# Two operand tiles of a two-layer block move behind two others, and every product operand starts at a multiple of 512 bytes

## The chip, the cores and the metric

The kernel runs on one core of one Trainium2 chip. The metric is the device time of one execution in microseconds (us). The engines are TensorE (PE: matrix products; PEld: its loads of the stationary operand), VectorE (DVE), ScalarE (ACT), GpSimd (POOL) and SyncE (SP, which here issues the DMAs). SBUF is the on-chip memory from which the engines read; a tile takes the same range of bytes in each of its 128 partitions, and "byte n" below means byte n of each partition.

## The reference, cut to what matters

Two layers, each a mixer (recurrence, two kinds of attention) and a gated feed-forward part, over 256 tokens of width 2048:

```python
for l in range(DEPTH):                                # 2
    h = rmsnorm(x, g_mix[l])
    proj = h @ w_in[l]                                # 2048 -> 3904
    ...                                               # out_a, out_b, out_c from proj
    x = x + concatenate([out_a, out_b, out_c]) @ w_out[l]
    h = rmsnorm(x, g_ffn[l])
    x = x + (silu(h @ w_gate[l]) * (h @ w_up[l])) @ w_down[l]   # 2048 -> 5632 -> 2048
return rmsnorm(x, g_final)
```

All inputs are float32. The weights are read once, 387 MB in all.

## The kernel before

**Products.** A float32 product is made of three products of a reduced type (F32R): each operand is split into a high part, rounded to that type, and a low part, the rest. `mm3` (L207) issues the three: high by high (L209), high by low (L210 or L211) and low by high. Each is a load of a 128x128 stationary operand and a stream of 512 (or 256, 320, 384) columns of the moving operand. TensorE's order is written out by hand (`manual_schedule`); the other engines' work is ordered by a scheduler around it.

**The operands.** Weights come by DMA from SP into `wraw` (three buffers of 4,096 bytes), `load_split` (L186) has ACT write the high part `whi` (L203) and DVE the low part `wlo` (L204), three buffers of 4,096 bytes each. The activations lie transposed, split in the same way, in one of two pairs: `xTh` and `xTl` (16 slices of 1,024 bytes each, one for 128 rows of width; written by `build_xT` at L292 and L293) hold the normed input of w_in, w_gate and w_up; `hTh` and `hTl` (six buffers of 4,096 bytes each) hold the mixer's output for w_out and the hidden units for w_down.

**Who is stationary.** In `gemm` (L213) a 128x128 slice of xT or hT is stationary and 512 columns of `whi` or `wlo` move. In `gemm_T` (L253) a 128x128 slice of `whi` or `wlo` is stationary and 256 columns of xT or hT move. In the profile the moving tile is named first: `acc<-whi,xTh` has `whi` moving and `xTh` stationary.

**The loop.** The feed-forward part takes 11 blocks of 512 hidden units: for each, w_gate and w_up are read in loads of 512 KB (two slices of 128 rows by 512 columns), and each load feeds 12 products of 512 columns. After blocks 6 and 11, w_down is read in loads of 512 KB (128 rows by 1024 columns), which feed 12 products of 512 columns too. Between these products stand a few transposes on TensorE (L283).

**Where tiles lie.** Pools are laid out one behind the other in the order in which they are opened: `const`, `wraw`, `whl` (`whi`, `wlo`), `ht` (`hTh`, `hTl`), `sm`. Within `const` tiles lie in the order of their allocation, each begun at a multiple of 32 bytes. `xTh` and `xTl` are tiles of `const`, behind `half` and ahead of a 68,240 byte work area (`arena`).

Of the kernel before, what the change touches and what calls it, by code (L numbers as in the profile page):

```python
# [11 lines left out]
F32 = mybir.dt.float32  # L12
F32R = mybir.dt.float32r
# [8 lines left out]
P = 128  # L22
D = 2048
T = 256
NT = 2
DEPTH = 2
KD = D // P
# [27 lines left out]
def body(ctx: ExitStack, tc: tile.TileContext, x_in, pos_in, pvec_in, lamv_in, cst_in, w_in, w_r, w_i, w_q_b,  # L55
         w_kv_b, w_out, w_gate, w_up, w_down, g_final, out):
    nc = tc.nc
    pool = lambda name, bufs=1, **k: ctx.enter_context(tc.tile_pool(name=name, bufs=bufs, **k))
    const = pool("const")
    wraw_p = pool("wraw", 3)  # L60
    whl_p = pool("whl", 3)
    ht_p = pool("ht", 6)
    sm_p = pool("sm", 4)
    acc_p = pool("acc", 5, space=PSUM)
    aux_p = pool("aux", 3, space=PSUM)
# [11 lines left out]
    load_x(0, 256)  # L77
    nc.sync.dma_start(pv, pvec_in)

    half = const.tile([P, 8], F32, name="half")  # L80
    xTh = const.tile([P, KD, T], F32R, name="xTh")
    xTl = const.tile([P, KD, T], F32R, name="xTl")
    junk = const.tile([P, 512], BF16, name="junk")
    warm = const.tile([P, 512], BF16, name="warm")
    nc.vector.memset(warm, 0.0)
    nc.gpsimd.memset(half, -0.5)
    nc.scalar.activation(junk[:, 0:8], half, AF.Exp)
    pos_i = const.tile([P, NT], I32, name="pos_i")
    cst = const.tile([P, 40], F32, name="cst")
    rsb = const.tile([P, T], F32, name="rsb")  # L90
# [833 lines left out]
```

## Time and profile before

| | |
|---|---|
| time, three runs | 2161.57, 2165.28, 2165.72 us; median 2165.28 us |
| profiled execution: its own time | 2164.01 us |
| profiled execution: its span | 2162.2 us |
| PE busy | 2146.5 us (99% of the span) |
| DVE, ACT, POOL busy | 1157.1, 1003.4, 12.9 us |
| mean DMA rate | 181 GB/s |

The span runs from the first to the last instruction of the program; the time has 1.8 us more around it. PE's busy time counts a product from its start to its modelled end. Products overlap: one of 512 columns is shown as 0.39 us long, but the next starts about 0.23 us after it. So what TensorE takes for a product is read from the distance between starts, and a mean duration serves to compare products of the same shape.

### The profile page before, as it was taken

The numbers are of one execution on the slowest core, as the hardware profiler recorded it, in microseconds if no ns is written. First come the engines' busy times: TensorE is split into PE (matmuls) and PEld (weight loads), VectorE is DVE, ScalarE is ACT, GpSimd is POOL, SyncE is SP. The second block draws the span as 40 slices with busy tenths as digits, with TensorE's granted clock in tenths as the row PEclk, the third lists the DMA queues.
The fourth block names the chain that finished last, engine by engine and source line by source line (L and its number), as shares of the span: only waits on it lengthen the run. The fifth ranks groups of instructions, "written<-read, shape, count | busy, mean of one in ns | idle before, by whom it ended". The sixth has DMA issues, their size and how long they took to land.

```text
span 2162.2 us, 26714 instructions
## 1 busy us (share of the span) xinstructions
PE 2146.5 (99%) x10302; PEld 1783.7 (82%) x10302; DVE 1157.1 (54%) x1497; ACT 1003.4 (46%) x1345; POOL 12.9 (1%) x27
## 2 busy tenths in 40 slices
PE   9999999999999999999999999999999999999998
PEld 8888888888888888888898888888888888888886
DVE  5775755444444444444565757554444444445454
ACT  5764654444443344443447546454444433444443
POOL 0000000000000000000000000000000000000000
PEclk9999999999999999999999999999999999999999
DMA  7564456666665666666565645566666666666655
GB/s 216 172 166 131 151 176 185 185 185 184 185 189 192 193 186 186 185 186 191 181 189 158 180 126 184 178 179 190 182 185 187 191 193 189 186 187 181 189 184 171
DMA packets 183439, 391.14 MB, mean 181 GB/s; under 512 B 19088, under 2 KB 36624, under 8 KB 183184
## 3 DMA queue, kind: packets, MB, share of 16 engines
q1 hardware_dynamic: 183312, 389.45, 60.7%
q8 instruction: 80, 1.31, 0.3%
q14 instruction: 47, 0.39, 0.1%
HBM read 387.30 MB, written 2.10 MB: 180 GB/s over the span
## 4 chain that ended last, share of the span: by engine, by line
PE 98%; DMA 0%; issue 0%; ACT 0%; DVE 0%; SPq 0%; DVEq 0%; POOLq 0%; POOL 0%; ACTq 0%
PE acc L209 31%; PE acc L211 31%; PE acc L210 31%; PE aux L283 2%; PE aux L676 1%; PE aux L675 1%; PE aux L732 1%; DMA wraw<-in_w_in 0%; PE aux L690 0%; PE aux L534 0%; PE aux L533 0%; ACT whi L203 0%; PE aux L691 0%; SPq L75 0%; DVE wlo L204 0%
## 5 line engine op out<-in xcount | busy, mean ns | idle before, releaser
L204 DVE TENSOR_TENSOR wlo<-wraw,whi 128x1024 fp32r<-128x1024 f32 (+2 forms) x756 | 895.4, 1185 | 880.1 <-ACT whi L203 879.0
L203 ACT CAST whi<-wraw 128x1024 fp32r<-128x1024 f32 (+2 forms) x756 | 770.1, 1019 | 1053.4 <-PE acc L211 934.5
L209 PE MATMUL acc<-whi,xTh 128*128 128x512 f32 x1728 | 685.1, 396 | 1.8 <-ACT whi L203 1.0
L210 PE MATMUL acc<-wlo,xTh 128*128 128x512 f32 x1728 | 676.8, 392 | 0.6 <-DVE wlo L204 0.6
L211 PE MATMUL acc<-whi,xTl 128*128 128x512 f32 x1728 | 676.8, 392 | 0.0
L209 PE MATMUL acc<-whi,hTh 128*128 128x512 f32 (+1 forms) x992 | 388.6, 392 | 0.0
L209 PEld LDWEIGHTS acc<-whi,xTh 128*128 128x128 f32 x1728 | 326.1, 189 | 74.8 <-issue 1.3
L211 PEld LDWEIGHTS acc<-whi,xTl 128*128 128x128 f32 x1728 | 325.8, 189 | 73.4
L211 PE MATMUL acc<-whi,hTl 128*128 128x512 f32 (+1 forms) x992 | 385.5, 389 | 0.0
L210 PEld LDWEIGHTS acc<-wlo,xTh 128*128 128x128 f32 x1728 | 326.2, 189 | 71.4 <-DVE wlo L204 0.9
L210 PE MATMUL acc<-wlo,hTh 128*128 128x512 f32 (+1 forms) x992 | 384.8, 388 | 0.0
L209 PEld LDWEIGHTS acc<-whi,hTh 128*128 128x128 f32 x992 | 186.8, 188 | 38.1 <-issue 1.3
L211 PEld LDWEIGHTS acc<-whi,hTl 128*128 128x128 f32 x992 | 186.5, 188 | 38.0
L210 PEld LDWEIGHTS acc<-wlo,hTh 128*128 128x128 f32 x992 | 186.8, 188 | 36.9
L209 PE MATMUL acc<-xTh,whi 128*128 128x256 f32 x384 | 110.6, 288 | 0.2 <-ACT whi L203 0.2
L211 PE MATMUL acc<-xTh,wlo 128*128 128x256 f32 x384 | 108.4, 282 | 0.8 <-DVE wlo L204 0.8
L210 PE MATMUL acc<-xTl,whi 128*128 128x256 f32 x384 | 108.2, 282 | 0.6 <-DVE xTl L293 0.6
L209 PEld LDWEIGHTS acc<-xTh,whi 128*128 128x128 f32 x384 | 72.4, 188 | 2.7 <-issue 1.3
L210 PEld LDWEIGHTS acc<-xTl,whi 128*128 128x128 f32 x384 | 72.4, 189 | 1.1 <-DVE xTl L293 1.0
L211 PEld LDWEIGHTS acc<-xTh,wlo 128*128 128x128 f32 x384 | 72.3, 188 | 1.2 <-DVE wlo L204 1.2
L826 DVE SCALAR_TENSOR_TENSOR arena<-acc,rs,arena 128x512 f32<-128x512 f32 x44 | 32.9, 748 | 42.9 <-PE acc L211 42.9
L283 PE MATMUL aux<-ident,arena 128*128 128x128 f32 x324 | 48.6, 273 | 0.0
(174 smaller groups left out, 868.1 us busy)
## 6 DMA issues: line engine op xcount, KB each, us to landing
wraw<-in_w_gate SPq DMA_DIRECT2D x176, 512.0 KB, 3.7
wraw<-in_w_up SPq DMA_DIRECT2D x176, 512.0 KB, 3.7
wraw<-in_w_down SPq DMA_DIRECT2D x176, 512.0 KB, 4.5
wraw<-in_w_out SPq DMA_DIRECT2D x64, 512.0 KB, 3.8
wraw<-in_w_in SPq DMA_DIRECT2D x64, 384.0 KB, 3.2
wraw<-in_w_in SPq DMA_DIRECT2D x48, 512.0 KB, 3.8
wraw<-in_w_in SPq DMA_DIRECT2D x32, 416.0 KB, 3.4
wraw<-in_w_q_b SPq DMA_DIRECT2D x8, 384.0 KB, 4.0
```

Of the source, the lines that this page charges most:

```text
L203: nc.scalar.copy(hi[:, :n], raw[:, :n])
L204: nc.vector.tensor_tensor(lo[:, :n], raw[:, :n], hi[:, :n].bitcast(F32), ALU.subtract)
L209: nc.tensor.matmul(ps, a[0], b[0], start=start, stop=False)
L210: nc.tensor.matmul(ps, a[0], b[1], start=False, stop=False)
L211: nc.tensor.matmul(ps, a[1], b[0], start=False, stop=stop)
L283: nc.tensor.transpose(ps[:, d:d + P], s, ident)
L675: nc.tensor.matmul(S[:, c0:c0 + n], qT[:, h, qs], kT[:, h, 0:n], start=True, stop=False)
L676: nc.tensor.matmul(S[:, c0:c0 + n], qrT[b0:b0 + 64, h // 2, qs], krT[b0:b0 + 64, 0:n], start=False, stop=True)
L732: nc.tensor.matmul(S[:, c0:c0 + n], qk[b0:b0 + 64, 0, q * P:(q + 1) * P], qk[b0:b0 + 64, 1, 0:n], start=True, stop=True)
L826: nc.vector.scalar_tensor_tensor(sil[t], ps, rs[0][:, t:t + 1], sil[t], ALU.mult, ALU.mult)
```

## The change

`xTh` and `xTl` leave `const` for a pool of their own, `xt`, which is opened behind `ht` and ahead of `sm`. `half` is allocated two tiles later, and a new tile `pad` of 32 bytes is allocated in `const` and set to zero on POOL.

```diff
     ht_p = pool("ht", 6)
+    xt_p = pool("xt")
     sm_p = pool("sm", 4)
...
-    half = const.tile([P, 8], F32, name="half")
-    xTh = const.tile([P, KD, T], F32R, name="xTh")
-    xTl = const.tile([P, KD, T], F32R, name="xTl")
+    xTh = xt_p.tile([P, KD, T], F32R, name="xTh")
+    xTl = xt_p.tile([P, KD, T], F32R, name="xTl")
     junk = const.tile([P, 512], BF16, name="junk")
     warm = const.tile([P, 512], BF16, name="warm")
     nc.vector.memset(warm, 0.0)
+    half = const.tile([P, 8], F32, name="half")
     nc.gpsimd.memset(half, -0.5)
     nc.scalar.activation(junk[:, 0:8], half, AF.Exp)
+
+    pad = const.tile([P, 8], F32, name="pad")
+    nc.gpsimd.memset(pad, 0.0)
```

The built programs place the tiles as follows (first byte of the first buffer; the buffers of one name follow each other at multiples of 4,096 bytes, and all slices that a product reads begin at multiples of 512 bytes within them):

| tile | before | rest of 512 | after | rest of 512 |
|---|---|---|---|---|
| `xTh` | 34,144 | 352 | 192,512 | 0 |
| `xTl` | 50,528 | 352 | 208,896 | 0 |
| `arena` | 70,176 | 32 | 37,440 | 64 |
| `wraw` | 139,232 | 480 | 106,496 | 0 |
| `whi` | 151,520 | 480 | 118,784 | 0 |
| `wlo` | 163,808 | 480 | 131,072 | 0 |
| `hTh` | 176,096 | 480 | 143,360 | 0 |
| `hTl` | 200,672 | 480 | 167,936 | 0 |

On PE, DVE, ACT and SP the two programs have the same instructions in the same order. POOL has one more. At the start of the program POOL's rows before are, with `ident` the unit matrix for the transposes and `arena` the work area:

```order
masks.py:197 MEMSET ident 128x128
L86 MEMSET half 128x8
L455 MEMSET arena 128x6x3
masks.py:199 ISA
masks.py:199 AFFINE_SELECT ident<-ident 128x128
```

and of the changed kernel:

```order
masks.py:197 MEMSET ident 128x128
L87 MEMSET half 128x8
L91 MEMSET pad 128x8
L459 MEMSET arena 128x6x3
masks.py:199 ISA
masks.py:199 AFFINE_SELECT ident<-ident 128x128
```

The zeroing of `pad` stands ahead of the last step of `ident`.

## Rows read from the trace of the kernel before

**Rows 1.** The page: busy us, share of the span and instructions of each engine.
```profile
PE 2146.5 (99%) x10302; PEld 1783.7 (82%) x10302; DVE 1157.1 (54%) x1497; ACT 1003.4 (46%) x1345; POOL 12.9 (1%) x27
```

**Rows 2.** The page: the chain that ended last, shares of the span by engine.
```profile
PE 98%; DMA 0%; issue 0%; ACT 0%; DVE 0%; SPq 0%; DVEq 0%; POOLq 0%; POOL 0%; ACTq 0%
```

**Rows 3.** Groups by line and form, TensorE: shapes, count | busy us, mean ns | idle before.
```profile
L209 PE MATMUL acc<-whi,xTh 128*128 128x512 f32 x1664 | 665.2, 400 | 1.8 <-ACT whi L203 1.0 <-DVE arena L487 0.8
L211 PE MATMUL acc<-whi,xTl 128*128 128x512 f32 x1664 | 657.0, 395 | 0.0
L210 PE MATMUL acc<-wlo,xTh 128*128 128x512 f32 x1664 | 656.8, 395 | 0.6 <-DVE wlo L204 0.6
L209 PE MATMUL acc<-whi,hTh 128*128 128x512 f32 x960 | 377.7, 393 | 0.0
L211 PE MATMUL acc<-whi,hTl 128*128 128x512 f32 x960 | 374.8, 390 | 0.0
L210 PE MATMUL acc<-wlo,hTh 128*128 128x512 f32 x960 | 374.1, 390 | 0.0
```

**Rows 4.** Windows, TensorE, w_down, then w_gate and w_up: busy (count), clock, DMA share, GB/s.
```profile
650.00:690.00 40.00, 40.00 (x178) 1.00 0.60 192
755.00:795.00 40.00, 40.00 (x174) 1.00 0.65 184
```

**Rows 5.** Timeline, TensorE, w_out, hT stationary: start us, length us, line.
```profile
311.67 0.39 PE L209 MATMUL acc<-whi,hTh 128*128 128x512 f32 x1
...
313.94 0.39 PE L210 MATMUL acc<-wlo,hTh 128*128 128x512 f32 x1
```

**Rows 6.** Timeline, TensorE, w_in, xT stationary.
```profile
1235.80 0.40 PE L210 MATMUL acc<-wlo,xTh 128*128 128x512 f32 x1
1236.04 0.40 PE L211 MATMUL acc<-whi,xTl 128*128 128x512 f32 x1
...
1238.14 0.39 PE L211 MATMUL acc<-whi,xTl 128*128 128x512 f32 x1
```

**Rows 7.** Timeline, TensorE, w_down, hT stationary, just after a group of transposes.
```profile
622.28 0.39 PE L210 MATMUL acc<-wlo,hTh 128*128 128x512 f32 x1
...
624.13 0.39 PE L209 MATMUL acc<-whi,hTh 128*128 128x512 f32 x1
```

**Rows 8.** Timeline and window, TensorE, a stretch at half clock.
```profile
263.27 0.63 PE L209 MATMUL acc<-whi,hTh 128*128 128x512 f32 x1
...
265.40 0.63 PE L211 MATMUL acc<-whi,hTl 128*128 128x512 f32 x1
...
263.00:265.60 2.60, 2.60 (x8) 0.50 0.51 170
```

**Rows 9.** Groups by line and form, TensorE: 256 columns of xT or hT moving.
```profile
L209 PE MATMUL acc<-xTh,whi 128*128 128x256 f32 x384 | 110.6, 288 | 0.2 <-ACT whi L203 0.2
L211 PE MATMUL acc<-xTh,wlo 128*128 128x256 f32 x384 | 108.4, 282 | 0.8 <-DVE wlo L204 0.8
L210 PE MATMUL acc<-xTl,whi 128*128 128x256 f32 x384 | 108.2, 282 | 0.6 <-DVE xTl L293 0.6
L209 PE MATMUL acc<-hTh,whi 128*128 128x256 f32 x72 | 20.7, 287 | 0.0
L210 PE MATMUL acc<-hTl,whi 128*128 128x256 f32 x72 | 20.4, 283 | 0.0
L211 PE MATMUL acc<-hTh,wlo 128*128 128x256 f32 x72 | 20.4, 283 | 0.0
```

**Rows 10.** Waits: who waited for whom, us in total, times, longest.
```profile
ACT whi L203 <- PE acc L211: 934.5, 561, 4.7
```

**Rows 11.** Timeline of the start: POOL's last step of ident, the first transpose.
```profile
0.87 0.10 POOL L86 MEMSET half<- 128x8 f32 x1
...
1.06 0.29 POOL masks.py:199 TENSOR_SCALAR_AFFINE_SELECT ident<-ident 128x128 f32<-128x128 f32 x1
...
3.34 0.45 PE L283 MATMUL aux<-ident,x 128*128 128x128 f32 x1
```

## The prediction

> **What bounds the kernel now.** I read first the busy times and the chain that ended last: TensorE is busy in 99% of the span and holds 98% of the chain [rows 1, 2]. No other engine's wait ends last over any stretch that counts, so the time changes by what TensorE's products change, and by nothing else unless a new wait appears.
>
> Then the groups by line and form. They show that equal work costs unequal time. A product of 512 columns takes 400, 395 and 395 ns on average in the three lines of `mm3` where a slice of xT is stationary, and 393, 390 and 390 ns where a slice of hT is [rows 3]. Nearly nothing stands idle ahead of either, so this is not waiting for a load.
>
> These durations overlap, so the distance of starts must bear it out, and it does in two ways. Two stretches of 40 us without transposes hold 178 products (hT, w_down) and 174 (xT, w_gate and w_up), both at a granted clock of 1.00, which is 2.4 GHz [rows 4]; about two in each count only reach in over an edge, which leaves 40/176 = 227 ns and 40/172 = 233 ns for one. And single starts, in two other stages: ten products of w_out with hT take 313.94 - 311.67 = 2.27 us, 227 ns each [rows 5]; ten of w_in with xT take 1238.14 - 1235.80 = 2.34 us, 234 ns each, the widest 0.24 us apart [rows 6].
>
> Last a stretch at a granted clock of 0.50 (1.2 GHz): there five products with hT take 265.40 - 263.27 = 2.13 us, 426 ns each [rows 8]. If the array alone set the pace, the full clock would give half of that, 213 ns. It gives 227 with hT and 233 or 234 with xT. So at the full clock 14 ns of each product (hT) and some 20 ns (xT) are not columns passing through the array. They vanish when the array is slower, so they look like waiting for operands; that is my reading, no row names it. These 14 to 20 ns are all that an edit of addresses can touch.
>
> **What differs between xT and hT.** Both are read in slices of 512 bytes per partition, at the same moment relative to the moving stream, in stages with the same 12 products for each load of 512 KB. What differs is where they begin. The moving `whi` and `wlo` begin at rest 480, the remainder of the first byte divided by 512. hT begins at rest 480 too, xT at rest 352. xT also lies below the work area, some 117 kB from `whi`, hT right behind `wlo`. The change makes xT like hT in both respects: all rests are equal, and xT lies behind hT, at addresses where `hTl` lay before. Whichever of the two accounts for the difference goes away.
>
> **The change part by part.**
>
> *xT stationary, 512 columns.* Three products cost (665.2 + 657.0 + 656.8)/1664 = 1189.3 ns with xT and (377.7 + 374.8 + 374.1)/960 = 1173.5 ns with hT [rows 3]. The hT figure already has in it the stretches just after transposes, where hT does no better than xT for a while: eight products in 624.13 - 622.28 = 1.85 us, 231 ns each [rows 7]. Gain: 15.8 ns x 1664 = 26.2 us. By the windows (233 - 227 = 6 ns for each of 4992) it would be 30; I take 26.2, which rests on all products and not on two stretches.
>
> *xT moving, 256 columns.* Here `whi` or `wlo` is stationary. Three products cost (110.6 + 108.4 + 108.2)/384 = 852.1 ns with xT and (20.7 + 20.4 + 20.4)/72 = 854.2 ns with hT [rows 9]. Becoming like hT costs 2.1 ns x 384 = 0.8 us.
>
> *xT stationary, 320 columns.* 64 triples without a counterpart: between nothing and 64 x 15.8 ns = 1.0 us. I take nothing.
>
> *hT against the weights.* Their rests are equal before and after (480, then 0). Nothing in the trace shows a product at rest 0. The bounds are below, as rivals; I take no change, because what would set the pace is how the two reads lie to each other, and that stays.
>
> *The supply.* Faster products ask for loads faster: 12 x 233 = 2.80 us for 512 KB becomes 2.72. The w_down stage already runs at that pace, at 192 GB/s, without its TensorE waiting [rows 4], and ACT's casts spend 934.5 us waiting for TensorE to give a buffer back [rows 10]: loads are ahead of TensorE. Cost: nothing. If this cover were gone, the DMA share of 0.65 would have to pass 1, that is one product in under 0.65 x 233 = 151 ns.
>
> *`pad` on POOL.* One instruction like that of `half`, 0.10 us, in front of the last step of `ident`, which ends at 1.35 us; the first transpose starts at 3.34 [rows 11]. Hidden with 2 us to spare; uncovered it would cost 0.1 us.
>
> Sum: -26.2 + 0.8 = -25.4 us. Against the profiled execution's own time, 2164.0 us, which lies 1.3 us under the median of the three runs: 2164.0 - 25.4 = 2138.6 us.
>
> **A rule of the skill against it.** The rows show that the place of the stationary operand matters to the stream that runs meanwhile (227 against 233 ns). The Trainium skill, "TensorE: Matmul & The Clock Gate", section "Step-by-step: what each phase is for", says that TensorE has two independent SBUF read ports and that loading the next weights takes no read bandwidth from the running product. By that rule the sum is 0 and the time 2164 us, the first rival below; this trace disagrees with it so far, by 15.8 ns for three products.
>
> **The rivals.**
>
> *Same.* The difference comes from something else that separates the xT stages from the hT stages, such as transfers in rows of 2 KB instead of 4 KB, or evacuations on other engines. Then moving tiles does nothing: 2164 us, within 2160 to 2168. For it: xT and hT are never used in the same stage. Against: xT has 234 and 233 ns in w_in and in w_gate and w_up, whose evacuations differ, and hT has 227 in both w_out and w_down [rows 4 to 6].
>
> *More than hT's pace.* The 14 ns that hT still loses come from beginning at rest 480, 32 bytes short of a multiple of 512, and go at rest 0. If all of it goes, 3 x (1664 + 960) = 7872 products of 512 columns save 14 ns each, 110 us [rows 3], and 3 x (384 + 72) = 1368 of 256 columns at most as much, 19 us [rows 9]: 2139 - 129 = 2010 us. If half goes: 2074 us. For it: the surplus is the memory's, and every operand here begins off such a multiple. Against: xT moving, from rest 352, is by 2.1 ns in three products quicker than hT moving from rest 480 [rows 9], so the surplus follows how two operands lie to each other, not how far one is from a multiple. The Trainium skill, "SBUF — State Buffer", section "Specifications (TRN2)", gives SBUF lines of 16 bytes; all starts are multiples of 32 already, so by that page this rival gains nothing. No row here shows a line's size.
>
> *Slower.* Both reads now begin on the very same boundary, and start nearly together for every product. If hT's even pace rests on the 32 bytes that were left ahead of the boundary, it is lost, and all products run in an uneven rhythm as xT does now. With hT at xT's pace and xT unchanged: 960 x 15.8 ns = +15.2 us, 2179 us. With every product at the widest distance, 0.24 us [rows 6]: 4992 x 7 ns + 2880 x 13 ns = +72 us, 2236 us. It decides as soon as hT loses more than xT wins, that is at over 27 ns for three products of hT if xT reaches hT's old pace, or at any loss if xT stays. For it: just after transposes hT runs at 231 ns [rows 7], so equal rests alone do not give the even pace at once. Against: over a whole stretch it does come, at 227 [rows 4].
>
> **How the numbers follow.** Forecast (xT takes hT's pace, 2130 to 2148): 0.53. More than that (2010 to 2130): 0.18, nearer the half than the whole. Same: 0.13. Slower: 0.16. About 0.2% (4.3 us) is what a measurement of this kernel can tell from no change. Faster is the first two, 0.71; same 0.13; slower 0.16. The predicted time is the forecast's, 2138.6 us. For the range I reach down to 2060, which takes in half of the surplus and a little more, and up to 2178, the mild end of slower. Left out are the deep gain (about 0.07) and most of slower (about 0.13).
>
> **What would show it.** Right: the three rows with xT stationary at about 393, 390 and 390 ns; the rows with hT unchanged; starts in a w_gate stretch 227 ns apart and even; 178 products in 40 us there; the loads' rate up by 2%. More than that: hT's rows fall too, and starts come near 213 to 220 ns. Same: all six rows as they are [rows 3]. Slower: hT's rows rise to 395 and more. Wrong in another way: TensorE waits for `whi` or `wlo`, which [rows 3] hardly show now.

## The result

The changed kernel takes 2139.93 us (median of four runs, 2138.0 to 2143.27), the kernel before 2164.28 us. The ratio is 0.9893 with a 95% interval of 0.988 to 0.9905: 1.1% faster, and 1.3 us over the 2138.6 us that were forecast. The profiled execution of the changed kernel took 2138.0 us, 26.0 us less than that of the kernel before; its span is 2136.2 us.

The page of the changed kernel: TensorE's busy time has gone down by 25.3 us against [rows 1], the other engines' is as it was within 1.2 us, and TensorE still holds the chain. The mean DMA rate rose from 181 to 183 GB/s.

```profile
PE 2121.2 (99%) x10302; PEld 1780.0 (83%) x10302; DVE 1157.0 (54%) x1497; ACT 1004.6 (47%) x1345; POOL 13.0 (1%) x28
...
PE 98%; DMA 1%; issue 0%; ACT 0%; SPq 0%; DVE 0%; DVEq 0%; POOLq 0%; POOL 0%; ACTq 0%
```

The groups by line and form (shapes, count | busy us, mean ns | idle before) show where. The lines are four further down than before: L213 to L215 are the three products of `mm3`.

```profile
L213 PE MATMUL acc<-whi,xTh 128*128 128x512 f32 x1664 | 657.6, 395 | 1.0 <-DVE arena L491 0.8 <-ACT whi L207 0.2
L215 PE MATMUL acc<-whi,xTl 128*128 128x512 f32 x1664 | 649.4, 390 | 0.0
L214 PE MATMUL acc<-wlo,xTh 128*128 128x512 f32 x1664 | 648.8, 390 | 0.6 <-DVE wlo L208 0.6
L213 PE MATMUL acc<-whi,hTh 128*128 128x512 f32 x960 | 377.0, 393 | 0.0
L215 PE MATMUL acc<-whi,hTl 128*128 128x512 f32 x960 | 374.0, 390 | 0.0
L214 PE MATMUL acc<-wlo,hTh 128*128 128x512 f32 x960 | 373.7, 389 | 0.0
...
L213 PE MATMUL acc<-xTh,whi 128*128 128x256 f32 x384 | 111.0, 289 | 0.6 <-ACT whi L207 0.6
L214 PE MATMUL acc<-xTl,whi 128*128 128x256 f32 x384 | 108.8, 283 | 0.6 <-DVE xTl L297 0.6
L215 PE MATMUL acc<-xTh,wlo 128*128 128x256 f32 x384 | 108.7, 283 | 0.5 <-DVE wlo L208 0.5
```

The three rows with xT stationary fell from 400, 395 and 395 ns [rows 3] to 395, 390 and 390. Those with hT stayed within 1 ns. Nothing new stands in the idle column.

The distance of starts says the same. In the timeline of a w_gate stage (start us, length us, line) twelve products with xT stationary take 451.36 - 448.64 = 2.72 us, 226.7 ns each, the distances all 0.22 or 0.23 us:

```profile
448.64 0.39 PE L213 MATMUL acc<-whi,xTh 128*128 128x512 f32 x1
448.86 0.39 PE L214 MATMUL acc<-wlo,xTh 128*128 128x512 f32 x1
449.09 0.39 PE L215 MATMUL acc<-whi,xTl 128*128 128x512 f32 x1
449.32 0.39 PE L213 MATMUL acc<-whi,xTh 128*128 128x512 f32 x1
...
451.36 0.39 PE L213 MATMUL acc<-whi,xTh 128*128 128x512 f32 x1
```

Summed over all starts of the two traces, from each product to the next instruction on TensorE: products with xT stationary and 512 columns took 1170.3 us before and 1146.3 after (-24.0); with hT stationary 659.4 and 657.9 (-1.5); all others together 0.5 less. That is the whole change of the span. In 40 us of w_gate and w_up the changed kernel has 178 products (740 to 780 us), where the kernel before had 174 in the same window.

### The profile page after: what moved, and what is told of

Read it like the earlier page. It is cut to its first block, busy times and chain, and to the rows that moved or that the text cites. A ratio compares the mean times of both kernels' runs of the same rounds, so it can differ in the third digit from the quotient of the medians.

```text
span 2136.2 us, 26715 instructions
## 1 busy us (share of the span) xinstructions
PE 2121.2 (99%) x10302; PEld 1780.0 (83%) x10302; DVE 1157.0 (54%) x1497; ACT 1004.6 (47%) x1345; POOL 13.0 (1%) x28
## 4 chain that ended last, share of the span: by engine, by line
PE 98%; DMA 1%; issue 0%; ACT 0%; SPq 0%; DVE 0%; DVEq 0%; POOLq 0%; POOL 0%; ACTq 0%
PE acc L213 31%; PE acc L215 31%; PE acc L214 31%; PE aux L287 2%; DMA wraw<-in_w_in 1%; PE aux L680 1%; PE aux L679 1%; PE aux L736 1%; PE aux L694 0%; PE aux L538 0%; PE aux L537 0%; ACT whi L207 0%; PE aux L695 0%; DVE wlo L208 0%; SPq L76 0%
## 5 line engine op out<-in xcount | busy, mean ns | idle before, releaser
L207 ACT CAST whi<-wraw 128x1024 fp32r<-128x1024 f32 (+2 forms) x756 | 771.7, 1021 | 1027.9 <-PE acc L215 904.7
L213 PE MATMUL acc<-whi,xTh 128*128 128x512 f32 x1728 | 677.4, 392 | 1.0 <-DVE arena L491 0.8
L214 PE MATMUL acc<-wlo,xTh 128*128 128x512 f32 x1728 | 668.6, 387 | 0.6 <-DVE wlo L208 0.6
L215 PE MATMUL acc<-whi,xTl 128*128 128x512 f32 x1728 | 669.1, 387 | 0.0
L213 PE MATMUL acc<-whi,hTh 128*128 128x512 f32 (+1 forms) x992 | 387.9, 391 | 0.0
L215 PE MATMUL acc<-whi,hTl 128*128 128x512 f32 (+1 forms) x992 | 384.7, 388 | 0.0
L213 PEld LDWEIGHTS acc<-whi,xTh 128*128 128x128 f32 x1728 | 325.0, 188 | 67.0 <-issue 1.3
L215 PEld LDWEIGHTS acc<-whi,xTl 128*128 128x128 f32 x1728 | 324.8, 188 | 66.6
L213 PEld LDWEIGHTS acc<-whi,hTh 128*128 128x128 f32 x992 | 186.4, 188 | 37.9 <-issue 1.3
L215 PEld LDWEIGHTS acc<-whi,hTl 128*128 128x128 f32 x992 | 186.2, 188 | 38.0
L213 PE MATMUL acc<-xTh,whi 128*128 128x256 f32 x384 | 111.0, 289 | 0.6 <-ACT whi L207 0.6
L215 PE MATMUL acc<-xTh,wlo 128*128 128x256 f32 x384 | 108.7, 283 | 0.5 <-DVE wlo L208 0.5
L213 PEld LDWEIGHTS acc<-xTh,whi 128*128 128x128 f32 x384 | 73.6, 192 | 2.5 <-issue 1.3
L215 PEld LDWEIGHTS acc<-xTh,wlo 128*128 128x128 f32 x384 | 73.5, 192 | 0.7 <-DVE wlo L208 0.7
```

What stands on the lines that cost most here:

```text
L207: nc.scalar.copy(hi[:, :n], raw[:, :n])
L213: nc.tensor.matmul(ps, a[0], b[0], start=start, stop=False)
L214: nc.tensor.matmul(ps, a[0], b[1], start=False, stop=False)
L215: nc.tensor.matmul(ps, a[1], b[0], start=False, stop=stop)
```

## The experiments

The change does three things to the operands at once: xT moves behind hT, xT gets the same remainder of 512 bytes as the others, and that remainder becomes 0. The first four runs take these apart. "Rest" is the remainder of a first byte divided by 512, as above; a "triple" is the sum of the three mean durations of `mm3` with 512 columns, the number that the prediction was made with (before: 1189.3 ns with xT, 1173.5 with hT; after: 1175.4 and 1171.6). In all runs but the last two the program's instructions are the same in the same order on PE, DVE, ACT and SP.

**Equal rests without the move.** In the kernel before:

```diff
+    gapa = const.tile([P, 32], F32, name="gapa")     # 128 bytes, set to zero on POOL
     xTh = const.tile([P, KD, T], F32R, name="xTh")
     xTl = const.tile([P, KD, T], F32R, name="xTl")
+    gapb = const.tile([P, 96], F32, name="gapb")     # 384 bytes, likewise
```

> xT stays in the first pool, low and far from the weights, as before; 128 bytes ahead of it and 384 behind it make its rest 480, equal to that of whi, wlo, hTh and hTl. Theory A (equal rests of the two reads give the even pace): all of the gain, about 2140 us, xT rows at 395, 390, 390 ns. Theory B (it is the place behind hT, near the weights): no gain, about 2164 us, xT rows at 400, 395, 395 ns. Theory C (it is the multiple of 512 bytes itself): no gain either, about 2164 us.

Measured: 2140.29 us, ratio to before 0.9894 (0.9879 to 0.9909). The xT groups, which were 400, 395 and 395 ns:

```profile
L213 PE MATMUL acc<-whi,xTh 128*128 128x512 f32 x1664 | 657.3, 395 | 2.5 <-ACT whi L207 2.1 <-DVE arena L491 0.5
L215 PE MATMUL acc<-whi,xTl 128*128 128x512 f32 x1664 | 649.2, 390 | 0.0
L214 PE MATMUL acc<-wlo,xTh 128*128 128x512 f32 x1664 | 648.3, 390 | 0.6 <-DVE wlo L208 0.6
```

The whole gain is there, with xT 118 kB below the weights and nothing at a multiple of 512. Theories B and C fall.

**The move without equal rests.** In the changed kernel:

```diff
+    gapa = xt_p.tile([P, 96], F32, name="gapa")      # 384 bytes
     xTh = xt_p.tile([P, KD, T], F32R, name="xTh")
```

> The changed kernel with 384 bytes ahead of xTh in its pool: xT lies behind hT, but begins at rest 384, which is 128 bytes short of the rest of whi and wlo (0), as far as before (352 against 480). Theory A (equal rests): all of the gain is lost, about 2164 us, xT rows at 400, 395, 395 ns, hT rows unchanged at 393, 390, 389. Theory B (place): the gain stays, about 2140 us. Theory C (multiples of 512): lost for xT, about 2164 us.

Measured: 2162.5 us, 0.9999 (0.9989 to 1.0008). Against the kernel before nothing is left, and the xT groups are back:

```profile
L215 PE MATMUL acc<-whi,xTh 128*128 128x512 f32 x1664 | 664.9, 400 | 2.5 <-ACT whi L209 2.3 <-DVE arena L493 0.2
L217 PE MATMUL acc<-whi,xTl 128*128 128x512 f32 x1664 | 657.2, 395 | 0.0
L216 PE MATMUL acc<-wlo,xTh 128*128 128x512 f32 x1664 | 656.7, 395 | 0.6 <-DVE wlo L210 0.6
```

**No multiple of 512.** The changed kernel without `pad` (all rests 480), and with a `pad` of 384 bytes (all rests 352, where xT alone began before):

```diff
-    pad = const.tile([P, 8], F32, name="pad")
-    nc.gpsimd.memset(pad, 0.0)
```

> The changed kernel without the 32 byte tile pad: xT behind hT, and every part begins at rest 480 instead of 0. Theory A (equal rests) and theory B (place): as the changed kernel, about 2140 us, within 0.2%. Theory C (multiples of 512 bytes): gain lost, about 2164 us.

```diff
-    pad = const.tile([P, 8], F32, name="pad")
+    pad = const.tile([P, 96], F32, name="pad")
```

> The changed kernel with pad of 384 bytes instead of 32: xT behind hT, and every part begins at rest 352, where xT began before. Theory A (equal rests): about 2140 us, all rows as in the changed kernel. Theory D (rest 352 is itself a bad start for a stationary operand): xT and hT both at 400, 395, 395 ns, about 2180 us.

Measured: 2137.75 us (0.9886, 0.987 to 0.9903) and 2139.04 us (0.9889, 0.9874 to 0.9904). Both triples with xT are 1174.3 ns. The first group of each kernel, the one without `pad` first:

```profile
L211 PE MATMUL acc<-whi,xTh 128*128 128x512 f32 x1664 | 656.9, 395 | 1.4 <-DVE arena L489 0.8 <-ACT whi L205 0.7
```

```profile
L213 PE MATMUL acc<-whi,xTh 128*128 128x512 f32 x1664 | 656.9, 395 | 1.7 <-ACT whi L207 1.4 <-DVE arena L491 0.3
```

So 0, 480 and 352 are the same to within the intervals as long as all operands share them. `pad` is not needed, and rest 352 is no bad start in itself.

**The weights moved instead.** If it is how the two reads lie to each other, then hT must lose its pace too when only `whi` and `wlo` move. In the changed kernel:

```diff
     wraw_p = pool("wraw", 3)
+    gapa_p = pool("gapa")                            # holds one tile of 128 bytes
     whl_p = pool("whl", 3)
+    gapb_p = pool("gapb")                            # holds one tile of 384 bytes
     ht_p = pool("ht", 6)
```

> The changed kernel with whi and wlo moved 128 bytes up (a 128 byte tile ahead of their pool, 384 bytes behind it): their rest is 128, that of hT and xT stays 0, so both lie 128 bytes short of the weights, as xT alone did before. Theory A (equal rests of the two reads): xT and hT both lose the even pace: xT rows 400, 395, 395 ns, hT rows 400, 395, 395 ns instead of 393, 390, 389; 2164 + 960 x 15.8 ns = about 2179 us, 0.7% slower than the kernel before. Theory E (something about xT alone, hT is immune): 2164 us or less.

Measured: 2183.67 us, 1.0097 (1.0078 to 1.0115), some 5 us more than theory A gave: starts are 233.2 ns apart with xT and with hT, not the 232.4 that xT had before (how this average is taken is said with the last two experiments). The groups with hT, whose distance to the weights no run had changed so far:

```profile
L219 PE MATMUL acc<-whi,hTh 128*128 128x512 f32 x960 | 381.9, 398 | 0.0
L221 PE MATMUL acc<-whi,hTl 128*128 128x512 f32 x960 | 379.1, 395 | 0.0
L220 PE MATMUL acc<-wlo,hTh 128*128 128x512 f32 x960 | 379.1, 395 | 0.0
```

hT is not immune: its triple went from 1171.6 to 1187.6 ns. Theory E falls. This is the "slower" rival's price, come about by another way than its mechanism.

**How far, and in which period.** The changed kernel with xT shifted by a tile in front of it, as in the second experiment, of 256, 128, 32 and 64 bytes; and by 16 bytes:

```diff
-    xTh = xt_p.tile([P, KD, T], F32R, name="xTh")
-    xTl = xt_p.tile([P, KD, T], F32R, name="xTl")
+    xTw = xt_p.tile([P, 2 * KD * T + 8], F32R, name="xTw")
+    xTh = xTw[:, 4:4 + KD * T].rearrange("p (k t) -> p k t", k=KD)
+    xTl = xTw[:, 4 + KD * T:4 + 2 * KD * T].rearrange("p (k t) -> p k t", k=KD)
```

> The changed kernel with 256 bytes ahead of xTh: xT at rest 256, half way round, weights and hT at 0. Theory A1 (any unequal rest costs about the same): about 2164 us. Theory A2 (what counts is how far the two reads are apart within 512 bytes, and half way round is furthest): below 2140 us, xT starts closer than 227 ns, down to 214 (4992 products x 13 ns = 65 us, 2075 us). Theory A3 (equal rests are the best there is): between 2140 and 2190 us.

> The changed kernel with 128 bytes ahead of xTh: xT at rest 128, that is 128 bytes past the weights instead of 128 short of them. With xT stationary: theory A1 (any unequal rest costs the same): about 2164 us. Theory A2 (the side counts; in the products with 256 columns of xT moving, where the weights are the stationary ones and lay 128 past it, three products took 2 ns less than at equal rests): at most 2140 us.

> The changed kernel with 32 bytes ahead of xTh: xT at rest 32, the smallest shift that tiles can have. Theory A1 (only equal rests give the even pace): about 2164 us. Theory F (only the 64 or 128 byte piece in which a read begins counts): gain kept, about 2140 us.

> The changed kernel with 64 bytes ahead of xTh: xT at rest 64, weights and hT at 0. With 128 bytes either way the gain was gone and with 256 it was kept. Theory A256 (what counts is whether the rests of 256 are equal): 2164 us, xT rows 400, 395, 395 ns. Theory G (only an odd number of 128 byte steps, or a start inside a 64 byte piece, costs): about 2140 us.

> The changed kernel with xTh and xTl cut from one tile 32 bytes wider, 16 bytes past its start: xT at rest 16. Theory A256 (equal rests of 256 needed): about 2164 us. Theory H (reads within the same 32 bytes count as equal): about 2140 us.

Measured, with the changed kernel and the second experiment beside them (the times of 16 and 64 bytes are single runs, beside one of the kernel before of 2161.71 us; their groups carry the reading; 384 past the weights, in a period of 512, is 128 short of them):

| xT past the weights by | time, us | ratio to before | triple, xT stationary, 512 columns | triple, xT moving, 256 columns |
|---|---|---|---|---|
| 0 | 2139.9 | 0.9893 (0.988 to 0.9905) | 1175.4 ns | 855.5 ns |
| 16 | 2144.2 | | 1179.7 | 848.4 |
| 32 | 2166.2 | 1.0013 (1.0003 to 1.0023) | 1191.2 | 846.1 |
| 64 | 2169.5 | | 1191.4 | 846.9 |
| 128 | 2163.9 | 1.0002 (0.9993 to 1.0012) | 1189.4 | 852.6 |
| 256 | 2138.7 | 0.9884 (0.987 to 0.9899) | 1174.5 | 860.7 |
| 384 | 2162.5 | 0.9999 (0.9989 to 1.0008) | 1189.2 | 852.6 |

The groups with 256 bytes, and with 32:

```profile
L215 PE MATMUL acc<-whi,xTh 128*128 128x512 f32 x1664 | 657.1, 395 | 1.3 <-DVE arena L493 0.8 <-ACT whi L209 0.5
```

```profile
L215 PE MATMUL acc<-whi,xTh 128*128 128x512 f32 x1664 | 665.9, 400 | 1.2 <-DVE arena L493 0.8 <-ACT whi L209 0.5
...
L215 PE MATMUL acc<-xTh,whi 128*128 128x256 f32 x384 | 109.8, 286 | 0.8 <-ACT whi L209 0.8
```

256 bytes apart is as good as 0, and 128 either way is as bad as before. So of the shifts tried, the two reads must begin at the same remainder of 256 bytes, not of 512 (192 and 320 were not tried); the kernel before had xT and the weights 128 of 256 apart. 32 bytes lose all of it, 16 bytes about a quarter (4.3 of some 15 ns of a triple). No shift is clear of none for products of 512 columns: theory A2 falls on both of its runs, since with 256 bytes the pace after a while is the same 226.7 ns. Theory A1 fits 32, 64, 128 and 384 bytes and falls with 256; theories F and G fall. A256 is right for 64 bytes, and at 16 bytes neither A256 (2164 us) nor H (2140 us) came true: 2144.2 lies between.

**The 14 ns that are left.** With equal rests a product still takes 13 to 14 ns more than half of what it takes at half clock. Is that the load of the next stationary operand, which runs beside it? In the changed kernel the second of the three products loads half, then a quarter, of its stationary columns, so that part of the small term high by low is left out of the output:

```diff
-        nc.tensor.matmul(ps, a[0], b[1], start=False, stop=False)
+        if a[0].shape[-1] == P and b[1].shape[-1] == 512:
+            nc.tensor.matmul(ps[0:64], a[0][:, 0:64], b[1], start=False, stop=False)
+        else:
+            nc.tensor.matmul(ps, a[0], b[1], start=False, stop=False)
```

> The changed kernel, where of each three products of 512 columns the second (L214 in the changed kernel) loads only 64 of its 128 stationary columns, so half of the small term high by low is left out of the output. Its load runs while the first product streams. Theory S (the 14 ns above 213 are the load's own reads, taken from the stream in proportion to its bytes): the first product takes 220 instead of 227 ns, 2624 x 7 = 18 us less, about 2121 us. Theory T (a fixed price for each load): 227 ns as before, about 2140 us. Theory U (the second product with its half output is dearer for another reason): more than 2140 us.

> As the run before with 32 of 128 stationary columns in the second product; three quarters of that small term are left out. Theory S (reads in proportion): the first product takes 217 ns, about 2140 - 2624 x 10 = 2114 us. Theory T (fixed price): about 2140 us.

Measured: 2161.1 and 2169.2 us in single runs. Both slower than the changed kernel, where theory S had them 19 and 26 us quicker. The load did get shorter (timeline of the weight loads with half of the columns, start us, length us):

```profile
659.73 0.19 PEld L213 LDWEIGHTS acc<-whi,hTh 128*128 128x128 f32 x1
659.97 0.13 PEld L215 LDWEIGHTS acc<-wlo,hTh 128*64 128x64 f32 x1
660.20 0.19 PEld L218 LDWEIGHTS acc<-whi,hTl 128*128 128x128 f32 x1
```

but the products did not. All three got longer, the full ones too:

```profile
L213 PE MATMUL acc<-whi,xTh 128*128 128x512 f32 x1664 | 659.0, 396 | 1.6 <-ACT whi L207 1.5
L215 PE MATMUL acc<-wlo,xTh 128*64 128x512 f32 x1664 | 654.4, 393 | 0.6 <-DVE wlo L208 0.6
L218 PE MATMUL acc<-whi,xTl 128*128 128x512 f32 x1664 | 653.8, 393 | 0.0
```

For an average of starts, take here and below every distance from one product of 512 columns to the next with the same operand (xT or hT) stationary, without those over 300 ns. With xT, the product during whose stream the half load runs takes 228.9 ns instead of 227.5, the next 230.7 instead of 227.3, the third 230.1 instead of 227.4; with the quarter load 229.5, 232.9 and 231.0. Theories S and T both fall. The time is what theory U allowed, but not by its reason alone, as the two full products got longer too. The even pace needs not only equal rests: it was lost when one load in three became shorter. The edit also cuts the rows that the second product writes, and no run tells the two apart. What the 13 to 14 ns are stays open.

## Why the prediction was right, point by point

**The bound.** TensorE was and is 99% busy, and what its products saved is what the span lost (26.0 us in both).

**xT stationary, 512 columns: -26.2 us forecast.** Measured by the same reckoning: (657.6 + 649.4 + 648.8)/1664 = 1175.4 ns for a triple against 1189.3, 13.9 ns x 1664 = 23.1 us. By starts it is 24.0 us. The step is right in its mechanism and 2 to 3 us too large: it took hT's triple as it stood, 1173.5 ns, and xT came to 1.9 ns above it. The starts of the changed kernel show why. After transposes or other work on TensorE the first product takes 334 ns with xT (318 with hT) until the next starts, the ten behind it 230.8 (230.4), and from the twelfth on both take 226.7. xT's products are broken into 78 times and hT's 34, which is more often per product too (64 against 85 products for each break); in the changed kernel a stretch at half clock and a wait of 0.8 us, both near 50 us, fall on xT too. The uneven pace behind the breaks is part of what the change was to remove, and stays: leaving out breaks, waits and half clock, products with xT lost 27.9 us against a steady 226.7 ns before, and 4.2 us after. The prediction saw the slow start in [rows 7], and did not count the breaks.

**hT against the weights: no change forecast.** The triple is (377.0 + 374.0 + 373.7)/960 = 1171.6 ns, 1.9 ns less, worth 1.8 us. This is neither the multiple of 512 (rests 480 and 352 for all, third and fourth experiment, came out alike) nor the change at all. The profiled execution of the kernel before ran eight hT products near 263 us at half clock [rows 8], which cost 1.6 us more than at the full clock's pace; that of the changed kernel ran the same products at full clock. In both, TensorE had waited 0.8 us for ScalarE shortly before. The run with xT 128 bytes past the weights, with hT at rest 0, has the stretch again, and with it 1173.6 ns. Windows (busy, clock, DMA share, GB/s) of the changed kernel and of that run, and that run's first group with hT:

```profile
260.50:263.10 2.60, 2.60 (x13) 1.00 0.45 131
```

```profile
263.70:266.30 2.60, 2.60 (x8) 0.50 0.63 202
...
L215 PE MATMUL acc<-whi,hTh 128*128 128x512 f32 x960 | 377.7, 393 | 0.0
```

The forecast's base thus held 1.9 ns of a triple that had nothing to do with addresses.

**xT moving, 256 columns: +0.8 us forecast.** 855.5 ns against 852.1: +1.3 us by durations. By starts these products took 143.3 us before and 143.0 after, but this holds pauses that differ by chance; the distances up to 160 ns are 118.7 ns on average before and 119.9 after, which is +1.3 us again. The sign was right; in the kernel's time it can't be told from no change.

**xT stationary, 320 columns: nothing forecast, within 0 to 1.0 us.** By starts they took 29.4 us before and 29.1 after, 0.3 us less.

**The sum.** -25.4 us were forecast, -26.0 measured between the two profiled executions and -24.4 between the medians. That the total is so close is partly luck. 1.5 of the 26.0 us are hT's half clock, which no term held. And with hT's triple free of it, 1171.6 ns, the main term would have been 17.7 ns x 1664 = 29.5 us, further from the 23 to 24 measured: the stretch at half clock in the base made up for more than half of what was not counted.

**The supply.** TensorE waits for no load that it did not wait for before. ACT's casts still wait for TensorE to give buffers back, 904.7 us in place of 934.5 [rows 10] (waits: us in total, times, longest):

```profile
ACT whi L207 <- PE acc L215: 904.7, 556, 3.5
```

**`pad`.** Hidden, as said: POOL's last step of `ident` now ends at 1.38 us instead of 1.35, and the first transpose starts at 3.43 (timeline of the start). That start is not `pad`'s: the run with two such tiles more in the kernel before (first experiment) has it at 3.35, the kernel before at 3.34.

```profile
0.91 0.11 POOL L91 MEMSET pad<- 128x8 f32 x1
...
1.09 0.29 POOL masks.py:199 TENSOR_SCALAR_AFFINE_SELECT ident<-ident 128x128 f32<-128x128 f32 x1
...
3.43 0.45 PE L287 MATMUL aux<-ident,x 128*128 128x128 f32 x1
```

**The mechanism.** The prediction named two accounts of why xT was slower, its rest and its place, and noted that the change removes both. The first two experiments settle it: the rest, to the whole amount, and the place not at all. (By the table of places xT came to lie where both hTh and hTl lay before, not hTl alone; as the place counts for nothing, no term changes.) The prediction counted rests in 512 bytes; the shifts tried say 256. The prediction's own argument against "more than hT's pace", that the surplus follows how two operands lie to each other, holds: hT's surplus is the same at rests 0, 480 and 352. Its reading that the surplus goes when the array is slower rested on hT alone; the trace before has xT at half clock too, at the granted clock of 0.50, and there unequal rests cost nothing that shows: 0.43 us from start to start, as with hT.

```profile
52.09 0.63 PE L210 MATMUL acc<-wlo,xTh 128*128 128x512 f32 x1
52.52 0.63 PE L211 MATMUL acc<-whi,xTl 128*128 128x512 f32 x1
52.95 0.47 PE L209 MATMUL acc<-whi,xTh 128*128 128x320 f32 x1
```

Why the two reads have to begin alike at full clock is not shown; the account ends at the remainder.

**The rule against it.** The Trainium skill, "TensorE: Matmul & The Clock Gate", section "Step-by-step: what each phase is for", says that loading the next weights takes no read bandwidth from the running product. These runs disagree for this type of product: moving nothing but the stationary operand by 128 bytes changes the average of starts from 227.4 to 232.4 ns (xT shifted by 128 bytes against the changed kernel). That it is bandwidth which is taken is not shown either: a load half as long did not help.

**"Slower".** Its price was about right (2179 us forecast for hT at xT's pace, 2183.7 measured when that was brought about), its mechanism wrong: with all rests at 0 the steady pace is the 226.7 ns that hT had at rest 480.

## What to carry to other kernels

Where the same work on the busiest engine shows two durations, ask what differs between the operands before asking what differs between the stages: here two groups of equal shape stood some 5 ns apart in one table, and each ns was worth 5 us. Let the stationary and the moving operand of F32R products of 512 columns begin at the same remainder of 256 bytes; a tile of some bytes in front of one of them is enough, and neither their order in memory nor `pad` mattered here. Take the price from the group that already has the property wanted, count how often the steady stretch that it rests on is broken, and look whether one of the two groups ran at half clock.

## What the runs showed of the hardware that was not expected

The even pace looks like a state that a stream of products falls into, not a price of each: with equal rests it takes some eleven products after a break, with xT and hT alike, until starts are 226.7 ns apart, and with unequal rests of 32 bytes and more the uneven pace lasts (233 ns on average with the weights 128 bytes off, for xT and hT alike).

Reads that are 32 or 64 bytes apart are bad for 512 columns with xT stationary (1191 ns against 1175 for a triple) and good for 256 columns with xT moving (846 and 847 against 855.5; by starts up to 160 ns apart 117.1 and 117.4 against 119.9). The two uses of xT want different places. A second copy of the weights' buffers for the second use would be worth at most 384 x 9.4 ns = 3.6 us, an estimate from the table; it was not tried.

Loading half of the stationary columns in one product of three made the kernel some 21 us slower (2161.1 against 2139.9 us, a single run against a median), although each such load is shown shorter itself (0.13 against 0.19 us).
